# Broadcast rows of a half requested one half ahead, and the first stage's casts and low parts moved between ScalarE, GpSimd and VectorE

## The chip, the core and the metric

The kernel runs on one core of a Trainium2 chip (trn2). The core has five engines with instruction queues of their own: TensorE (PE in the rows, with its weight loads as PEld), VectorE (DVE), ScalarE (ACT), GpSimd (POOL) and SyncE (SP). All transfers between memory and the core's on-chip buffers are issued here from SyncE's queue. The metric is the device time of one execution in microseconds (us). The kernel before takes 1203.94 us, the median of three runs (1199.38 to 1205.58).

## The reference

A hybrid encoder layer is computed in float32 for two sequences, 512 and 256 tokens long, with 16 shared meta tokens in front of each. What matters for this change is the start: the layer norm, the input projection, and the preparation of the gated delta branch.

```
h = _layer_norm(concat(meta_tokens, x), ln_in_g, ln_in_b)      # 16 + 512 and 16 + 256 rows of 1024
proj = h @ w_in                                                # then split: c_q, c_kv, k_r, qkv, z, gates
qkv = silu(_centred_conv(qkv, conv_w)); q, k = _l2norm(q), _l2norm(k)
g, beta = -exp(a_log) * softplus(a + dt_bias), sigmoid(b)      # forward and backward
gc = cumsum(g) in chunks of 64;  decay = exp(gc_i - gc_j) below the diagonal
m = strict(k beta k^T * decay);  attn = (q k^T) * decay;  qg = q * exp(gc)
(solve with m + I per chunk, scan over the chunks, attention branch, w_out, feed-forward, two layer norms)
```

## The kernel before, in words

All 784 rows (16 meta, 512, 256) are handled together; the meta rows are computed once. The program is written as a sequence of loops, and a scheduler then fixes the order of the instructions on each engine from what they read and write; every engine, and SyncE's queue of transfers, works through its list in that order. Where a list stands at an instruction whose inputs or buffers are not ready, everything behind it on this engine waits.

First stage (lines 275 to 317). The rows are normalised in two halves, `s` = 0 and 1, of 400 and 384 rows. For each of eight slices `k` of 128 features TensorE transposes the slice (L308, L311), ScalarE applies gain and bias and writes `full` (called through `act`, L188), a cast writes the high part `hTh` (L316), and VectorE writes the low part `hTl = full - hTh` (L317). In the kernel before, the cast runs on VectorE for even `k` and on ScalarE for odd `k`. `hTh` and `hTl` together carry float32 accuracy through matrix multiplies of a narrower type.

Projection (`proj`, lines 320 to 333). A weight tile `wr` of 128 columns is loaded (L256), ScalarE casts it to its high part `wh` (L212), and the engine given as `eng` subtracts to its low part `wl` (L213). Then 48 matrix multiplies (L331) sum `wh*hTh + wh*hTl + wl*hTh`. In the kernel before, `eng` is GpSimd for the first projection (keys' rotary part and gates) and for the first pair of the delta branch, and VectorE for the pairs after it. `wh` and `wl` have two buffers each.

Gates (lines 338 to 431). The first projection's result is copied by ScalarE to `graw` (L346 to L349), VectorE forms `krt` (L350, L351), TensorE turns the gates (L354) and the rotary part (L437), VectorE computes the gate arithmetic, and rows of the result go to memory as `gD` (L420, L423).

Delta branch (lines 525 to 571). Four pairs of heads `j`; for each, two projections with convolution (`conv`, its sums on VectorE at L465), normalisation (`l2`), and a copy of the keys by tokens to `kt` (L508), which four transfers store to `vD` (L512). Then two halves, of seven chunks each. A half loads `x3`: five rows of `gD`, broadcast to 64 partitions, in two transfers (L542). `x3` has two buffers, so the load for a half waits until the half two before it has last read its own; that last reader is GpSimd's `ua` (L568). From `x3` VectorE forms `dc` (L547, L548), GpSimd masks it (L549, L550), ScalarE takes the exponential, and the products with the matrix multiplies of L561 are written to `LT` and, over three `ua` buffers, stored to `UD` (L571). Two stores belong to each `ua`.

What follows (the rest of the projections, the solve by chunks, the scan, attention, the output projection and the feed-forward) is not touched.

Of the kernel before, what the change touches and what calls it, by code (L numbers as in the profile page):

```python
# [5 lines left out]
F32 = mybir.dt.float32  # L6
# [7 lines left out]
P = 128  # L14
# [8 lines left out]
NCH = 14  # L23
# [114 lines left out]
def body(ctx, tc, I, O):  # L138
    nc = tc.nc
    V, S, G, T = nc.vector, nc.scalar, nc.gpsimd, nc.tensor  # L140
    ld = nc.sync.dma_start
# [108 lines left out]
    hTh = htp.tile([P, KT, NT], F32R, name="hTh")  # L250
# [24 lines left out]
    with ExitStack() as e0:  # L275
        xp = pool(e0, "xp", 1, "left")
        xs = pool(e0, "xs", 3, "left")
        xt = {}
        for t in (0, 1, 2, 3, 4, 5, 6):
            n = P if t else NM  # L280
            r0 = 0 if t == 0 else NM + (t - 1) * P
            x = xp.tile([n, D], F32, name=f"x{t}")
            ld(x, I["x"][r0:r0 + n, :])
            xt[t] = x
            if t == 3:
                ld(cst, I["consts"])
                ld(cols, I["cols"])
                w0 = load_w(0)
        m2 = xp.tile([P, 7, 2], F32, name="m27")
        G.memset(m2[:, 0], 1.0)  # L290
        for s, ts in enumerate((range(4), range(4, 7))):
            for t in ts:
                n = P if t else NM
                moments(xt[t], n, m2[:n, t], xs)
            tl = slice(ts[0], ts[-1] + 1)
            norm_factors(m2[:, tl], stat[:, tl], xs)
            for i, t in enumerate(ts):
                n = P if t else NM
                x, mv = xt[t], stat[:n, t]
                if i in (2,):  # L300
                    act(x, x, AF.Identity, bias=mv[:, 0:1], scale=mv[:, 1:2])
                else:
                    V.tensor_scalar(x, x, mv[:, 1:2], mv[:, 0:1], ALU.mult, ALU.add)
            for k in range(KT):
                ps = bank()
                ks = slice(k * P, (k + 1) * P)
                if s == 0:
                    T.transpose(ps[:, 0:NM], xt[0][:, ks], ident[:NM, :NM])  # L308
                o = 0 if s else NM
                for t in range(3):  # L310
                    T.transpose(ps[:, o + t * P:o + (t + 1) * P], xt[1 + s * 3 + t][:, ks], ident)  # L311
                w = H0 if s == 0 else HR
                cs = slice(s * H0, s * H0 + w)
                full = xs.tile([P, H0], F32, name="full", bufs=4)
                act(full[:, :w], ps[:, :w], AF.Identity, bias=col("lnb", k), scale=col("lng", k))
                (S.copy if k % 2 else V.tensor_copy)(hTh[:, k, cs], full[:, :w])  # L316
                V.tensor_sub(hTl[:, k, cs], full[:, :w], hTh[:, k, cs].bitcast(F32))  # L317


    def proj(ti, real=False, wr=None, eng=V):  # L320

        if wr is None:
            wr = load_w(ti)
        wh = wp.tile([P, KT, P], F32R, name="wh")
        wl = wp.tile([P, KT, P], F32R, name="wl")
        split(wr, wh, wl, eng=eng)
        ps = bank2()
        for s, (c0, c1) in enumerate(((NM if real else 0, H0), (H0, NT))):
            for k in range(KT):
                for i, (a, b) in enumerate(((wh, hTh), (wh, hTl), (wl, hTh))):  # L330
                    T.matmul(ps[:, s, :c1 - c0], lhsT=a[:, k, :], rhs=b[:, k, c0:c1],  # L331
                             start=(k == 0 and i == 0), stop=(k == KT - 1 and i == 2))
        return ps
# [1 line left out]

    eg = ExitStack()
    gp = pool(eg, "gp", 1, "left")
    ps = proj(0, wr=w0, eng=G)
    graw = gp.tile([P, GC], F32, name="graw")
    krt = gp.tile([64, NT], F32, name="krt")  # L340
    rk = gp.tile([64, NT], F32, name="rk")
# [10 lines left out]
    ps = bank()  # L352
# [42 lines left out]
    for nm, src in (("gcT", g), ("glT", g), ("bT", be)):  # L395
        o = gqp.tile([P, 2, 7, 2, 4], F32, name=nm)
        for rho in range(2):
            ps = bank()
            rows = slice(rho * 64, rho * 64 + 64)
# [12 lines left out]
    gD = dp.tile([2, 5, 56, 64], F32, name="gD")  # L412
    for i, src in enumerate((gcT[:, 0], gcT[:, 1], nbT[:, 0])):
        ps = bank()
# [19 lines left out]
    ps = bank2()  # L434
# [17 lines left out]
    def conv(ti, wi, eng=V, ceng=V):  # L452

        ps = proj(ti, eng=eng)
        xb = xbs[cnt[0] % 2]
        cnt[0] += 1
        S.copy(xb[:, 1:401], ps[:, 0, :H0])
        S.copy(xb[:, 532:548], ps[:, 0, 0:NM])
        S.copy(xb[:, 401:529], ps[:, 1, 0:128])
        S.copy(xb[:, 548:804], ps[:, 1, 128:HR])  # L460
        y = ps.rearrange("p a c -> p (a c)")[:, 0:803] if wi < 8 else ytile()
        S.mul(y, xb[:, 0:803], col("cw", wi * 4))
        for i in (1, 2, 3):
            if ceng is V:
                V.scalar_tensor_tensor(y, xb[:, i:i + 803], col("cw", wi * 4 + i), y, ALU.mult, ALU.add)  # L465
            else:
                t = ceng.tile([P, 803], F32, name="vt", bufs=2)
                S.mul(t, xb[:, i:i + 803], col("cw", wi * 4 + i))
                G.tensor_add(y, y, t)
        return y  # L470

    es = ExitStack()
    sp = pool(es, "sp", 1)
# [45 lines left out]
    def zgate(j):  # L519
# [2 lines left out]
        act(z[:, :NR].rearrange("p (a c) -> p a c", a=2), ps[:, :, :HR], AF.Silu)  # L522
        st(zD[j], z[:, :NR])

    for j in range(NPB):
        yk = conv(1 + 2 * j, 4 + j, eng=V if j else G)
        yq = conv(2 + 2 * j, j, eng=V if j else G)
        kq = sp.tile([P, 2, NCH, 64], F32, name="kq", bufs=2)
        ks, qs = (silu_pad(y, sp.tile([P, GC], F32, name="ks", bufs=2)) for y in (yk, yq))
        l2(ks, kq[:, 0], None)  # L530
        l2(qs, kq[:, 1], 0.125)
        tokens(kq[:, 0].rearrange("p n c -> p (n c)"), sp.tile([P, GC], F32, name="kt"), j, 0, bank)
        for half in range(2):
            n0 = half * 7
            ch = slice(n0, n0 + 7)
            rows = slice(j * NCH + n0, j * NCH + n0 + 7)

            x3 = sp.tile([P, 5, 7, 64], F32, name="x3", bufs=2)
            en = x3[:, 3:5]
            for h in range(2):  # L540
                hr = slice(h * 64, h * 64 + 64)
                ld(x3[hr].rearrange("p r n c -> p r (n c)"),  # L542
                   gD[h, :, rows].rearrange("r n c -> r (n c)").partition_broadcast(64))

            dc = sp.tile([P, 4, 7, 64], F32, name="dc", bufs=2)
            gc = bc(gcT[:, :, ch, j], 3, 64)
            V.tensor_sub(dc[:, 1:4:2], x3[:, 0:2], gc)  # L547
            V.tensor_sub(dc[:, 2], gc[:, 1], x3[:, 1])  # L548
            G.tensor_add(dc[:, 1:3], dc[:, 1:3], bc(bc(C("nf"), 1, 7), 1, 2))  # L549
            G.tensor_add(dc[:, 3], dc[:, 3], bc(C("nb"), 1, 7))  # L550
            act(dc[:, 1:4], dc[:, 1:4], AF.Exp)
            act(en, en, AF.Exp)
            G.tensor_mul(dc[:, 0], x3[:, 2], dc[:, 1])
            V.tensor_mul(dc[:, 2], dc[:, 2], bc(nbT[:, 1, ch, j], 2, 64))
            b = bds[half]
            S.copy(b[0:64, :, 64:128], kq[0:64, 0, ch, :])
            S.copy(b[64:128, :, 0:64], kq[64:128, 0, ch, :])
            for a, w in ((0, 4), (4, 3)):
                ps = bank()
                for i in range(w):  # L560
                    T.matmul(ps[:, i * P:(i + 1) * P], lhsT=b[:, a + i, :],  # L561
                             rhs=kq[:, :, n0 + a + i, :], start=True, stop=True)
                p4 = ps[:, :w * P].rearrange("p (n a c) -> p a n c", a=2, c=64)
                sl = slice(a, a + w)
                nj = slice((n0 + a) * 4 + j, (n0 + a + w - 1) * 4 + j + 1, 4)
                V.tensor_mul(LT[:, :, nj, :], bc(p4[:, 0], 1, 2), dc[:, 0:4:2, sl])
                ua = sp.tile([P, 2, 4, 2, 64], F32, name="ua", bufs=3)
                G.tensor_mul(ua[:, :, :w, 0, :], en[:, :, sl], bc(kq[:, 1, n0 + a:n0 + a + w, :], 1, 2))  # L568
                V.tensor_mul(ua[:, :, :w, 1, :], bc(p4[:, 1], 1, 2), dc[:, 1:4:2, sl])
                for r in range(2):  # L570
                    st(UD[r, n0 + a:n0 + a + w, :, j].rearrange("n p i c -> p n (i c)"), ua[:, r, :w].rearrange("p n i c -> p n (i c)"))  # L571
# [10 lines left out]
    for i0 in range(0, 64, 4):  # L582
        ps = bank()
# [141 lines left out]
    for i0 in range(0, 32, 4):  # L725
        ps = bank()
# [6 lines left out]
    for h in range(2):  # L733
        for b in range(2):
            rows = slice(h * 64 + b * 32, h * 64 + b * 32 + 32)
# [5 lines left out]
    for n0, r in ((0, 0), (96, 1), (16, 0), (80, 1), (32, 0), (64, 1), (48, 0), (56, 1)):  # L741
        w = 8 if n0 in (48, 56) else 16
# [15 lines left out]
        for h in range(2):  # L758
            rows = slice(h * 64 + 32, h * 64 + 64)
# [9 lines left out]
        for h in range(2):  # L769
            o = h * 64 + (32 if r else 0)  # L770
            R = slice(o, o + 32)
            c = 0 if r else 32
# [21 lines left out]
    for i in range(NBD):  # L794
        for l, nm in ((TBs, "TB"), (WBs, "WB"))[:2 if i < 2 else 1]:
            t = us.tile([P, 4, P], F32, name=f"{nm}{i}")
            for h in range(2):
                c = (1 - h) * 64 if nm == "TB" else h * 64
# [105 lines left out]
    for i in range(len(order) + 2):  # L904
        for _ in range(1):
            next(latg, None)
        if i < len(order):
            c, step = order[i]
# [5 lines left out]
        if i >= 2:  # L914
            c, step = order[i - 2]
# [4 lines left out]
            n = chains[c][1][step]  # L920
# [107 lines left out]
    for s in range(2):  # L1028
        ps = bank("v")
# [3 lines left out]
    for j in range(NPB):  # L1033
        for s in range(2):
            ps = bank("v")
            cs = slice(s * HR, (s + 1) * HR)
# [326 lines left out]
```

## Time and profile before

| | |
|---|---|
| median of three runs | 1203.94 us (1199.38 to 1205.58) |
| the profiled execution's own time | 1201.35 us |
| its span in the profile | 1199.4 us |
| mean granted TensorE clock | 0.967 of full speed |
| TensorE matrix multiplies busy | 1123.9 us, 94% of the span |
| VectorE busy | 831.6 us, 69% |
| ScalarE busy | 598.9 us, 50% |
| GpSimd busy | 156.6 us, 13% |

The span is the time from the first to the last instruction of one execution. A row of the timeline gives a start in us from the span's start, how long the instruction (or several alike, "x3") took, the engine, the line, and what is written from what; in brackets stands how long the engine was idle before it and what ended the wait. The chain that ended last follows the work back from the last instruction, at each step to what released it; it names, stretch by stretch, who was waited for. The rows by windows give each engine's busy time in a stretch, then the granted clock, the share of the transfer engines and GB/s.

### The profile page before, as it was taken

How to read it: one execution, taken by the hardware profiler on the slowest of the kernel's cores; microseconds unless marked ns; L12 is line 12 of the kernel's file. 1: busy time of each engine (PE TensorE's matmuls, PEld its weight loads, DVE VectorE, ACT ScalarE, POOL GpSimd, SP SyncE). 2: the span in 40 equal slices, each digit the busy share in tenths (PEclk: the TensorE clock that was granted, in tenths of full speed). 3: DMA queues.
4: the chain of work that ended last, by engine and by line, in shares of the span. 5: the costliest groups of instructions: out<-in, count | busy, mean ns of one | idle time of the engine just before them, and what ended most of it. 6: DMA issues, size and time to landing. Idle time of an engine off the chain costs nothing.

```text
span 1199.4 us, 18635 instructions
## 1 busy us (share of the span) xinstructions
PE 1123.9 (94%) x7116; PEld 974.5 (81%) x7116; DVE 831.6 (69%) x1358; ACT 598.9 (50%) x1054; POOL 156.6 (13%) x195
## 2 busy tenths in 40 slices
PE   5978888998999899998999899999998999999997
PEld 4877788998889876664677789999998888888885
DVE  7567668689677768778648699777764764494446
ACT  5475664333745656656534566555553533343330
POOL 2134465004513211000000000000000000000000
PEclk9998899999899989899999899999999999999999
DMA  5157764530478764334103025333324875566521
GB/s 209 50 117 182 196 171 130 126 113 31 146 253 238 214 188 124 102 98 158 45 18 106 18 71 179 129 123 123 124 88 145 306 229 177 176 206 203 179 91 52
DMA packets 107962, 168.94 MB, mean 141 GB/s; under 512 B 36242, under 2 KB 72850, under 8 KB 107874
## 3 DMA queue, kind: packets, MB, share of 16 engines
q1 hardware_dynamic: 107874, 167.76, 45.7%
q8 instruction: 56, 0.92, 0.3%
q14 instruction: 32, 0.26, 0.1%
HBM read 128.61 MB, written 39.11 MB: 140 GB/s over the span
## 4 chain that ended last, share of the span: by engine, by line
PE 77%; DVE 9%; DMA 6%; ACT 4%; issue 2%; SPq 1%; POOL 1%; DVEq 0%; ACTq 0%; POOLq 0%
PE w L1326 15%; PE w L1084 10%; PE b L1084 9%; PE d L331 7%; PE b L1326 7%; PE b L1146 5%; PE d L977 3%; PE c L1008 3%; DMA x<-gD 3%; PE b L837 2%; PE d L704 2%; PE b L853 2%; PE v L1005 2%; PE b L877 2%; PE b L870 2%
## 5 line engine op out<-in xcount | busy, mean ns | idle before, releaser
L1326 PE MATMUL w<-w2h,fh 128*128 128x512 f32 x768 | 185.1, 391 | 3.8 <-ACT fh L212 3.8
L1326 PEld LDWEIGHTS w<-w2h,fh 128*128 128x128 f32 x768 | 144.9, 189 | 34.3 <-ACT fh L212 4.1
L331 PE MATMUL d<-hTh,wl 128*128 128x384 f32 (+1 forms) x352 | 123.9, 352 | 3.3 <-DVE wl L213 3.3
L331 PE MATMUL d<-hTh,wh 128*128 128x384 f32 (+1 forms) x352 | 125.1, 355 | 1.4 <-ACT ks L188 1.4
L331 PE MATMUL d<-hTl,wh 128*128 128x384 f32 (+1 forms) x352 | 125.1, 355 | 0.0
L213 DVE TENSOR_TENSOR w2h<-LT,w2h 128x1024 fp32r<-128x1024 f32 x64 | 77.6, 1224 | 48.7 <-ACT w2h L212 48.7
L212 ACT CAST w2h<-LT 128x1024 fp32r<-128x1024 f32 x64 | 66.6, 1049 | 75.4 <-PE b L1326 28.8
L1326 PE MATMUL b<-w2h,fh 128*128 128x512 f32 x384 | 96.4, 389 | 0.0
L1326 PEld LDWEIGHTS b<-w2h,fh 128*128 128x128 f32 x384 | 72.3, 188 | 15.1
L331 PEld LDWEIGHTS d<-hTh,wh 128*128 128x128 f32 x352 | 67.6, 192 | 5.8 <-issue 3.3
L331 PEld LDWEIGHTS d<-hTh,wl 128*128 128x128 f32 x352 | 67.6, 192 | 5.8 <-DVE wl L213 3.7
L331 PEld LDWEIGHTS d<-hTl,wh 128*128 128x128 f32 x352 | 67.6, 192 | 2.6 <-issue 1.5
L213 DVE TENSOR_TENSOR fh<-fr,fh 128x768 fp32r<-128x768 f32 x32 | 30.5, 957 | 55.9 <-ACT fh L212 55.9
L212 ACT CAST fh<-fr 128x768 fp32r<-128x768 f32 x32 | 26.7, 839 | 76.0 <-PE w L1326 38.7
L212 ACT CAST w1h<-LT 128x512 fp32r<-128x512 f32 x50 | 30.8, 620 | 41.2 <-PE w L1084 20.9
L1146 PE MATMUL b<-woh,mh 128*128 128x512 f32 x96 | 42.2, 448 | 5.2 <-ACT woh L212 3.1
L977 PE MATMUL d<-kt,q 128*128 128x512 f32 (+1 forms) x96 | 46.6, 582 | 0.3 <-ACT p L188 0.2
L213 DVE TENSOR_TENSOR w1l<-LT,w1h 128x512 fp32r<-128x512 f32 x50 | 34.4, 689 | 12.6 <-ACT w1h L212 12.6
L1008 PE MATMUL c<-pt,vt 128*64 128x512 f32 (+3 forms) x96 | 42.2, 536 | 0.6 <-ACT pt L1007 0.6
L857 DVE TENSOR_TENSOR YZ<-U,b 64x512 f32<-64x512 f32 x52 | 35.5, 683 | 7.6 <-PE b L853 6.9
L834 ACT COPY YZ<-U 64x512 f32<-64x512 f32 x52 | 32.1, 617 | 17.3 <-issue 11.3
L978 DVE TENSOR_REDUCE mx<-d 128x1 f32<-128x512 f32 (+1 forms) x48 | 28.7, 599 | 16.7 <-PE d L977 16.5
(473 smaller groups left out, 2810.4 us busy)
## 6 DMA issues: line engine op xcount, KB each, us to landing
LT<-in_w_ff SPq DMA_DIRECT2D x85, 512.0 KB, 3.8
FD<-LT SPq DMA_DIRECT2D x16, 768.0 KB, 3.7
fr<-FD SPq DMA_DIRECT2D x32, 384.0 KB, 3.7
wr<-in_w_in SPq DMA_DIRECT2D x22, 512.0 KB, 3.5
x<-gD SPq DMA_DIRECT2D x16, 560.0 KB, 6.2
KV<-vD SPq DMA_DIRECT2D x26, 256.0 KB
U<-UD SPq DMA_DIRECT2D x26, 256.0 KB, 5.3
w1x<-in_w_ff SPq DMA_DIRECT2D x12, 512.0 KB, 4.5
```

Source lines behind the costliest of these rows:

```text
L212: S.copy(hi, src)
L213: return (eng or V).tensor_sub(lo, src, hi.bitcast(F32))
L331: T.matmul(ps[:, s, :c1 - c0], lhsT=a[:, k, :], rhs=b[:, k, c0:c1], start=(k == 0 and i == 0), stop=(k == KT - 1 and i == 2))
L704: T.matmul(ps[:, s, :HR], lhsT=a[:, k], rhs=b[:, cs], start=(k == 0 and i == 0), stop=(k == 2 and i == 2))
L834: S.copy(YZ[h][rows], U[rows, :, :, 1])
L857: V.tensor_sub(YZ[h][rows], U[rows, :, :, 0], wv[rows])
L977: T.matmul(ps[:, :w], lhsT=q[:, qs], rhs=kt[:, k0:k0 + w], start=True, stop=True)
L978: V.tensor_reduce(mx[:, 0, t:t + 1], ps[:, :w], AX.X, ALU.max)
L1008: T.matmul(po[:m, :nq], lhsT=Vs[j][:, t0 + bi, :m], rhs=pt[:, :nq], start=(bi == 0), stop=(bi == ntl - 1))
L1084: x = T.matmul(ps[:, :HR], lhsT=a[:, k, :], rhs=b[:, k, :], start=(k == 0 and i == 0), stop=(k == HQ - 1 and i == 2))
L1146: outp = T.matmul(ps, lhsT=x[:, k, :], rhs=y[:, cs], start=(k == 0 and i == 0), stop=(k == 3 and i == 2))
L1326: T.matmul(po[g][h], lhsT=a[:, i_, qs], rhs=b[:, cs], start=(n_ == 0 and j == 0), stop=(n_ == len(seq) - 1 and j == 2))
```

## The change

Three things are edited. The cast to `hTh` runs on ScalarE for all eight slices. The low part `wl` of the first projection and of the first pair's two projections is formed on VectorE instead of GpSimd. And the loads of `x3` move into a function `lines`, which is called once before the loop for the first half and then, in each half, for the half that follows, in front of this half's own work and stores.

```
-                (S.copy if k % 2 else V.tensor_copy)(hTh[:, k, cs], full[:, :w])
+                S.copy(hTh[:, k, cs], full[:, :w])
...
-    ps = proj(0, wr=w0, eng=G)
+    ps = proj(0, wr=w0)
...
+    def lines(j, half):
+
+        rows = slice(j * NCH + half * 7, j * NCH + half * 7 + 7)
+        x3 = sp.tile([P, 5, 7, 64], F32, name="x3", bufs=2)
+        for h in range(2):
+            hr = slice(h * 64, h * 64 + 64)
+            ld(x3[hr].rearrange("p r n c -> p r (n c)"),
+               gD[h, :, rows].rearrange("r n c -> r (n c)").partition_broadcast(64))
+        return x3
+
+    x3n = lines(0, 0)
     for j in range(NPB):
-        yk = conv(1 + 2 * j, 4 + j, eng=V if j else G)
-        yq = conv(2 + 2 * j, j, eng=V if j else G)
+        yk = conv(1 + 2 * j, 4 + j)
+        yq = conv(2 + 2 * j, j)
...
-            x3 = sp.tile([P, 5, 7, 64], F32, name="x3", bufs=2)
+            x3 = x3n
             en = x3[:, 3:5]
-            for h in range(2):
-                hr = slice(h * 64, h * 64 + 64)
-                ld(x3[hr].rearrange("p r n c -> p r (n c)"),
-                   gD[h, :, rows].rearrange("r n c -> r (n c)").partition_broadcast(64))
+            if 2 * j + half < 7:
+                x3n = lines(j + half, 1 - half)
```

Since a scheduler sets the order, the lists of the built programs say what moves. ScalarE in the second half of the first stage, from the first `full` of 384 rows to the cast of the second weight pair; the list before:

```order
L188 ACTIVATE full<-b,cols 128x384 x4
L316 CAST hTh<-full 128x384
L188 ACTIVATE full<-b,cols 128x384
L316 CAST hTh<-full 128x384
L188 ACTIVATE full<-b,cols 128x384 x2
L316 CAST hTh<-full 128x384
L188 ACTIVATE full<-b,cols 128x384
L188 ACTIVATE ea<-gv 128x16
L316 CAST hTh<-full 128x384
L212 CAST wh<-wr 128x1024
```

Four casts stand among eight `full`. The list now, over the same stretch:

```order
L188 ACTIVATE full<-b,cols 128x384 x3
L316 CAST hTh<-full 128x384
L188 ACTIVATE full<-b,cols 128x384
L316 CAST hTh<-full 128x384 x3
L188 ACTIVATE full<-b,cols 128x384 x3
L316 CAST hTh<-full 128x384 x2
L188 ACTIVATE full<-b,cols 128x384
L316 CAST hTh<-full 128x384 x2
L188 ACTIVATE ea<-gv 128x16
L212 CAST wh<-wr 128x1024
```

Eight casts stand there, the last two right in front of the weight cast. In the first half ScalarE's list gains four casts in the same way, and VectorE's loses its four and gains two subtractions of `wl`; a third `wl` now stands on VectorE just ahead of `krt` (L350).

SyncE's queue in the delta branch, from the second half of pair `j` = 0 to pair 2; the names `x_994`, `x_1208` and `x_1243` are the `x3` of the second half of pair 1 and of the two halves of pair 2. The list before:

```order
L571 DMA UD<-ua 128x4x128 x2
L542 DMA x_994<-gD 64x5x448 x2
L256 DMA wr<-in_w_in 128x1024
L571 DMA UD<-ua 128x3x128 x2
L256 DMA wr<-in_w_in 128x1024 x2
L542 DMA x_1208<-gD 64x5x448 x2
L512 DMA vD<-kt 64x7x64 x4
L571 DMA UD<-ua 128x4x128 x2
L571 DMA UD<-ua 128x3x128 x2
L571 DMA UD<-ua 128x4x128 x2
L571 DMA UD<-ua 128x3x128 x2
L542 DMA x_1243<-gD 64x5x448 x2
```

The same stretch now, where `x_962`, `x_997` and `x_1211` are the three tiles, and L531 and L578 are the old L542 and L571:

```order
L578 DMA UD<-ua 128x4x128 x2
L531 DMA x_962<-gD 64x5x448 x2
L256 DMA wr<-in_w_in 128x1024
L578 DMA UD<-ua 128x3x128 x2
L256 DMA wr<-in_w_in 128x1024 x2
L512 DMA vD<-kt 64x7x64 x4
L531 DMA x_997<-gD 64x5x448 x2
L578 DMA UD<-ua 128x4x128 x2
L578 DMA UD<-ua 128x3x128 x2
L578 DMA UD<-ua 128x4x128 x2
L578 DMA UD<-ua 128x3x128 x2
L531 DMA x_1211<-gD 64x5x448 x2
```

The two loads for the first half of pair 2 stand behind the four stores of `vD`, where they stood in front of them. At every other place SyncE's queue has the order it had. Around the same place ScalarE's second copy to `kt` now precedes the first product of the convolution (L462), and on VectorE one sum of the convolution (L465) changes places with one pair of products (L566, L569). Beyond that the lists of all engines are the same but for a few neighbours.

## Rows read from the trace of the kernel before

**Rows 1.** Windows: length, busy PE, PEld, DVE, ACT, POOL, clock, DMA share, GB/s
```profile
12.00:25.00 13.00, 12.43 (x55) 9.99 (x56) 12.86 (x28) 9.19 (x18) 6.15 (x8) 1.00 0.48 175
25.00:35.00 10.00, 8.57 (x50) 6.64 (x49) 7.27 (x14) 8.00 (x15) 0.00 (x0) 1.00 0.07 18
...
38.60:40.80 2.20, 2.20 (x7) 2.11 (x7) 2.02 (x5) 0.79 (x2) 0.00 (x0) 0.50 0.69 225
...
184.00:260.00 76.00, 76.00 (x461) 74.77 (x461) 60.37 (x80) 32.54 (x56) 16.28 (x20) 0.98 0.52 135
```
**Rows 2.** Timeline of VectorE in the first half of the first stage
```profile
17.96 0.56 DVE L317 TENSOR_TENSOR hTl<-full,hTh 128x400 fp32r<-128x400 f32 x1
...
19.87 2.63 DVE L317 TENSOR_TENSOR hTl<-full,hTh 128x400 fp32r<-128x400 f32 x1
```
**Rows 3.** Timeline of GpSimd in the same stretch
```profile
18.83 3.24 POOL L213 TENSOR_TENSOR wl<-wr,wh 128x1024 fp32r<-128x1024 f32 x1 [3.17 <-ACT wh L212]
```
**Rows 4.** Line 316, all its instructions: ns min/median/max, first and last start
```profile
L316 DVE CAST hTh<-full x8: 301/360/540, 15.7 to 32.0; 128x400 fp32r<-128x400 f32 x4, 128x384 fp32r<-128x384 f32 x4
L316 ACT CAST hTh<-full x8: 516/524/532, 16.1 to 32.9; 128x400 fp32r<-128x400 f32 x4, 128x384 fp32r<-128x384 f32 x4
```
**Rows 5.** Timeline of VectorE, a weight's low part formed there
```profile
50.64 1.23 DVE L213 TENSOR_TENSOR wl<-wr,wh 128x1024 fp32r<-128x1024 f32 x1 [5.57 <-PE b L403]
```
**Rows 6.** Timeline of ScalarE, second half of the first stage
```profile
27.07 2.36 ACT L188 ACTIVATE full<-b,cols 128x384 f32<-128x384 f32 x4 [0.83 <-PE b L311]
29.31 0.52 ACT L316 CAST hTh<-full 128x384 fp32r<-128x384 f32 x1
29.71 0.69 ACT L188 ACTIVATE full<-b,cols 128x384 f32<-128x384 f32 x1
...
32.95 0.52 ACT L316 CAST hTh<-full 128x384 fp32r<-128x384 f32 x1
```
**Rows 7.** Chain that ended last, 31 to 40 us: start, length, what
```profile
31.00 3.57 PE d L331 x19
...
34.64 1.04 ACT wh L212
...
36.72 0.58 DVE krt L350
```
**Rows 8.** Timeline of SyncE's queue: start, issue time, transfer
```profile
101.61 1.47 SPq L542 DMA_DIRECT2D x<-gD  x2
...
126.56 1.25 SPq L542 DMA_DIRECT2D x<-gD  x2
127.92 3.03 SPq L512 DMA_DIRECT2D vD<-kt  x4
```
**Rows 9.** Timeline of ScalarE at the copies by tokens of pair 1
```profile
124.48 0.63 ACT L508 COPY kt<-b 128x512 f32<-128x512 f32 x1
...
125.82 0.53 ACT L508 COPY kt<-b 128x384 f32<-128x384 f32 x1
```
**Rows 10.** Timeline of VectorE at the arrival of broadcast rows
```profile
111.42 1.09 DVE L547 TENSOR_TENSOR dc<-x,gcT 128x896 f32<-128x896 f32 x1 [4.22 <-DMA x<-gD]
...
134.66 1.09 DVE L547 TENSOR_TENSOR dc<-x,gcT 128x896 f32<-128x896 f32 x1 [1.85 <-DMA x<-gD]
```
**Rows 11.** Timeline of GpSimd behind the arrival at 134.66
```profile
135.83 1.45 POOL L550 TENSOR_TENSOR dc<-dc,cst 128x448 f32<-128x448 f32 x1 [5.02 <-DVE dc L547]
137.51 1.01 POOL L568 TENSOR_TENSOR ua<-x,kq 128x384 f32<-128x384 f32 x1 [0.23 <-DMA UD<-ua]
```
**Rows 12.** Chain that ended last, 100 to 178 us: start, length, what
```profile
102.26 9.04 DMA x<-gD
...
140.73 7.86 DMA x<-gD
...
157.01 2.93 PE d L331 x8
...
170.02 7.20 DMA x<-gD
```

More of the change, by code (lines that the diff above doesn't have):

```diff
@@ L535, in body @@
             ch = slice(n0, n0 + 7)
-            rows = slice(j * NCH + n0, j * NCH + n0 + 7)
-            x3 = sp.tile([P, 5, 7, 64], F32, name="x3", bufs=2)
+            x3 = x3n
             en = x3[:, 3:5]
-            for h in range(2):
-                hr = slice(h * 64, h * 64 + 64)
-                ld(x3[hr].rearrange("p r n c -> p r (n c)"),
-                   gD[h, :, rows].rearrange("r n c -> r (n c)").partition_broadcast(64))
+            if 2 * j + half < 7:
+                x3n = lines(j + half, 1 - half)
             dc = sp.tile([P, 4, 7, 64], F32, name="dc", bufs=2)
```

## The prediction

> **What bounds the kernel now.** I read the page's busy times first: TensorE is at work for most of the span, so a change pays or costs only where TensorE is made to wait. Then the chain that ended last, for the stretch the edits touch. From 31 to 40 us it goes through TensorE's multiplies of the first projection (31.00, ending at 34.57), ScalarE's weight cast and VectorE's `krt` [rows 7]. From 100 to 178 us it goes three times through a load of broadcast rows, 9.04, 7.86 and 7.20 us long [rows 12]. Behind 184 us TensorE is busy for 76.00 of 76 us [rows 1]: what arrives there late stays late, for the lists fix the order and there is no pause to absorb a delay. Third I read the engines' timelines around these places, and last the built lists, which say what really moves.
>
> **First stage, first half.** Off VectorE go four casts of 0.36 us (1.4) [rows 4]. Off goes also a stall: one `hTl` took 2.63 us where its like takes 0.56 [rows 2], while GpSimd formed `wl` from 18.83 to 22.07 [rows 3]; with GpSimd empty that is 2.1 less. On it come two `wl` of 1.23 us, 2.5 [rows 5]. VectorE alone would reach the second half's normalisation, near 25 us, about 1.0 us sooner. ScalarE gets four casts of 0.52 us, 2.1, in a window in which it is idle for 13.00 - 9.19 = 3.8 us [rows 1, 4]; but the low part of the eighth slice waits for the last of them and stands in VectorE's list ahead of the last normalisation factor (L234). So the bounds are 1.0 us gained (ScalarE keeps up) and 2.1 us lost (none of its casts is hidden). I take a gain of 0.3, nearer to VectorE's own count, since ScalarE has idle time for all four casts.
>
> **First stage, second half.** Here ScalarE is the fuller engine, 8.00 of 10 us against VectorE's 7.27 [rows 1]. From 27.07 four `full` take 2.36, 0.59 each, and a cast delays what follows by 0.40, from 29.31 to 29.71 [rows 6]. Eight of each make 4.7 + 3.2 = 7.9 us, so the last cast ends at 35.0, where it ended at 33.47 [rows 6]. Behind it come one low part (0.56) and its two multiplies (0.2 each [rows 7]), so TensorE's first projection ends at 36.0, not 34.57: 1.4 us late. The bounds are 0 (TensorE late anyway) and 2.1 (four casts at full length). The third `wl` starts when the weight cast ends (34.64 + 1.04 = 35.68 [rows 7]) and now stands ahead of `krt` on VectorE; 35.68 + 1.23 = 36.9 against 36.72, another 0.2. If `krt` had to wait for it in full, 1.2. The first stage therefore loses 1.4 + 0.2 - 0.3 = 1.3 us. Its bounds are -1.0 and 2.1 + 2.1 + 1.2 = +5.4.
>
> The Trainium skill (Perfetto Trace Analysis, Optimizing Scalar/DVE Operations) speaks against this half of the edit: where VectorE has a fast mode for an operation it does it faster, and work is handed to ScalarE when VectorE is saturated. The trace agrees on the first part, 0.36 against 0.52 us [rows 4], and VectorE is not saturated in the second half, 7.27 of 10 us [rows 1]. By the rule the price would be the difference of the durations, four times 0.16 or 0.6 us; by the rows it is the whole length on ScalarE, since ScalarE ends last.
>
> **The broadcast rows.** The loads do not come a half earlier. SyncE's list keeps its order at seven of eight halves, as the scheduler had moved the loads up already, and a load still waits for GpSimd's last read of the tile two halves before. At the one other place, the first half of pair 2, the two loads fall behind the four stores of `vD`. The stores need the second copy to `kt`, which ended at 126.35 and now follows straight on the first: 125.11 and about 0.4 make 125.5 [rows 9]. Issuing the four takes 3.03 us [rows 8], so the loads go out at 128.6 instead of 126.56, 2.0 later. From the first issue to VectorE's first use it took 134.66 - 126.56 = 8.1 us [rows 8, 10]. The load at 101.61, which went out shortly behind four such stores, took 111.42 - 101.61 = 9.8 [rows 8, 10]. I take 8.1, since that load had two stores of `UD` ahead of it too; 9.8 would add 1.7. What waits: VectorE's `dc` at 134.66, GpSimd's mask behind it, and behind the mask in GpSimd's list the `ua` that frees `x3` for the second half of pair 2. The mask ended at 137.28 and `ua` started at 137.51, held by a store of `UD` [rows 11], so 0.2 of the 2.0 is hidden and the next load, on the chain at 140.73 [rows 12], goes out 1.8 us late. TensorE waits behind that one until 157.01. The bounds are 0 (the `UD` store hides it) and 1.8 + 1.7 = 3.5. The swaps around it (one sum of the convolution behind a pair of products) I cost at nothing: VectorE waits 1.85 us for the rows there already [rows 10], and loses at most a 1.09-us instruction if that cover goes.
>
> The Trainium skill (DMA: Bandwidth & Descriptors, Queues, rings and completion order) says that a transfer engine takes descriptors in the order of its ring. By this rule the loads would begin only when the data of the four stores is through, and this term would be the upper bound, 3.5 us and not 1.8. The load at 101.61 bears that out in part; its 9.8 us hold two more stores as well.
>
> **Sum.** 1.3 + 1.8 = 3.1 us later. On the profiled execution, 1201.35 us (1199.4 of span and 2 around it), that is 1204.5. The median of the runs is 2.6 above this execution, so the forecast is 1207, 0.26% above 1203.94. About 0.5%, 6 us, is what a measurement of this kernel can tell from no change; the forecast lies inside.
>
> **Rivals.** First, slower through TensorE's clock. After the pause behind 34.57 the granted clock was 0.50 from 38.6 to 40.8, the lower level of 1.2 GHz [rows 1], and at 157.01 eight multiplies took 2.93 us [rows 12] where 19 take 3.57, or 1.5 for eight [rows 7]: 1.4 us for one such stretch. All three new waits (behind the last cast, at the first half of pair 2, at the second) lengthen pauses of TensorE. If each brings one more slow stretch that multiplies wait on, 4.3 is added: 3.1 + 4.3, or 1211. It decides from two stretches on, 3.1 + 2.9 = 6.0. For it speaks that both pauses were followed by the low clock; against it, that these stretches are there already and may only shift.
>
> Second, the casts hide. If ScalarE keeps up in both halves, the first stage gains the 1.0 us of VectorE, and with the queue's 1.8 the sum is +0.8: 1205. For it speaks ScalarE's 3.8 idle microseconds in the first half; against it, the count in the second.
>
> Third, the change does what it says and the rows of a half are there when it begins. The three loads on the chain are worth 9.04 + 7.86 + 7.20 = 24.1 us [rows 12]; since the mask and the `UD` stores are late next, about half would come through: 1192. Against it stands SyncE's list.
>
> **How the numbers follow.** The forecast gets 0.49, the clock 0.20, the hidden casts 0.24, the earlier rows 0.07. Slower by over 0.5% (above 1210) is most of the clock's 0.20 and the upper end of the forecast's bounds, 0.21 together. Faster by over 0.5% (below 1198) is the third rival and a little of the second, 0.08. Within 0.5% is 0.71. The range starts from the forecast and the clock: with both terms near their upper bounds, or two slow stretches, 1212; with the first stage at its lower bound, no cost of the queue, and a median as much below 1203.94 as the profiled execution is, 1200. Beyond lie the earlier rows and three slow stretches together with large terms.
>
> **What would show it.** In the profile of the changed kernel no `hTl` takes over 0.7 us in the first half; ScalarE's last cast of the first stage ends near 35 us, and TensorE's first projection near 36. The two loads for pair 2 go out about 2 us after the first of the four `vD` stores would have let them, and VectorE waits longer at that `dc`. The chain still goes through three loads of broadcast rows of 7 to 10 us. The prediction is wrong if these loads leave the chain, if TensorE's first projection ends by 34.6, or if the second load of pair 2 is issued no later, counted from `kt`, than before.

## The result, and the profile after

The changed kernel took 1210.39 us (median of six executions), the kernel before, run beside it, 1202.07: a ratio of 1.006 [1.0034, 1.0085]. In a second series (e1 below) it took 1206.58 (twelve executions) against 1202.74: 1.0031 [1.0021, 1.0042]. By the ratios the change costs 7.2 us in the first series and 3.7 in the second. The forecast was 1207, 3.1 us later; the two intervals share only a narrow strip at 1.004, so the size is known to some 2 us, and the first median lies 3.4 above the forecast and inside its range. Ratios leave out the executions in which TensorE's clock was low throughout (0.56 in the profiled one of the six), so the rows below are those of a second profile, an execution of 1205.0 us with a span of 1203.0.

The first stage, ScalarE's timeline, beside [rows 6]:

```profile
26.97 1.80 ACT L188 ACTIVATE full<-b,cols 128x384 f32<-128x384 f32 x3 [0.82 <-PE b L311]
...
29.63 1.34 ACT L316 CAST hTh<-full 128x384 fp32r<-128x384 f32 x3
30.86 1.82 ACT L188 ACTIVATE full<-b,cols 128x384 f32<-128x384 f32 x3
...
33.92 0.96 ACT L316 CAST hTh<-full 128x384 fp32r<-128x384 f32 x2
```

ScalarE goes from cast to `full` to cast without a gap, and the last cast ends at 34.88; before, it ended at 33.47. VectorE's timeline, beside [rows 2]:

```profile
17.94 0.55 DVE L317 TENSOR_TENSOR hTl<-full,hTh 128x400 fp32r<-128x400 f32 x1
...
21.79 1.55 DVE L317 TENSOR_TENSOR hTl<-full,hTh 128x400 fp32r<-128x400 f32 x3 [0.56 <-ACT hTh L316]
24.22 0.58 DVE L317 TENSOR_TENSOR hTl<-full,hTh 128x400 fp32r<-128x400 f32 x1 [0.42 <-ACT hTh L316]
24.91 0.81 DVE L303 TENSOR_SCALAR x<-x,stat 128x1024 f32<-128x1024 f32 x1
```

The `hTl` of 2.63 us is gone, but VectorE now waits for ScalarE's casts, and the second half's normalisation starts at 24.91. In the kernel before that row reads

```profile
25.00 1.54 DVE L303 TENSOR_SCALAR x<-x,stat 128x1024 f32<-128x1024 f32 x2
```

so this execution gains 0.1 us in the first half; a second profile of the same kernel (e6) gains nothing. The chain of waits from 35 us, beside [rows 7]:

```profile
35.10 0.97 PE d L331 x4
...
36.10 1.05 ACT wh L212
...
38.32 0.57 DVE krt L350
```

The first projection ends at 36.07 (34.57 before), and `krt` starts 1.60 us later than before.

Then the transfers. SyncE's queue, beside [rows 8]:

```profile
128.81 2.96 SPq L512 DMA_DIRECT2D vD<-kt  x4
132.28 1.26 SPq L531 DMA_DIRECT2D x<-gD  x2
...
145.32 1.25 SPq L531 DMA_DIRECT2D x<-gD  x2
```

ScalarE, beside [rows 9]:

```profile
127.78 1.00 ACT L508 COPY kt<-b 128x512 f32<-128x512 f32 x2
```

The four stores go out as soon as the second copy is done, and the two loads follow half a microsecond behind them. Counted from the start of the first copy to `kt`, the loads go out after 4.50 us (132.28 - 127.78), before after 2.08 (126.56 - 124.48): 2.4 later. It is the stores that held them and not the buffer, whose last reader on GpSimd was done at 129.83:

```profile
126.69 3.14 POOL L575 TENSOR_TENSOR ua<-x,kq 128x512 f32<-128x512 f32 x2 [1.09 <-DVE kq L498]
```

VectorE's arrivals, beside [rows 10]:

```profile
114.71 1.09 DVE L554 TENSOR_TENSOR dc<-x,gcT 128x896 f32<-128x896 f32 x1 [4.83 <-DMA x<-gD]
140.73 1.09 DVE L554 TENSOR_TENSOR dc<-x,gcT 128x896 f32<-128x896 f32 x1 [4.25 <-DMA x<-gD]
154.05 1.09 DVE L554 TENSOR_TENSOR dc<-x,gcT 128x896 f32<-128x896 f32 x1 [2.69 <-DMA x<-gD]
```

GpSimd behind the second of them, beside [rows 11]:

```profile
141.90 1.47 POOL L557 TENSOR_TENSOR dc<-dc,cst 128x448 f32<-128x448 f32 x1 [7.52 <-DVE dc L554]
143.34 1.01 POOL L575 TENSOR_TENSOR ua<-x,kq 128x384 f32<-128x384 f32 x1
```

The wait at the first half of pair 2 grew from 1.85 to 4.25 us, and `ua` no longer waits for a store of `UD`. The chain, beside [rows 12], now goes through four loads:

```profile
104.90 9.69 DMA x<-gD
132.94 7.67 DMA x<-gD
145.94 7.98 DMA x<-gD
176.16 7.46 DMA x<-gD
```

### The profile page after: what moved, and what is told of

Same layout as the page of the kernel before. It is cut to its first block, busy times and chain, and to the rows that moved or that the text cites. A ratio compares the mean times of both kernels' runs of the same rounds, so it can differ in the third digit from the quotient of the medians.

```text
span 1823.8 us, 18636 instructions
## 1 busy us (share of the span) xinstructions
PE 1787.9 (98%) x7116; PEld 1216.5 (67%) x7116; DVE 829.8 (45%) x1353; ACT 605.1 (33%) x1062; POOL 144.0 (8%) x192
## 4 chain that ended last, share of the span: by engine, by line
PE 96%; DVE 1%; ACT 1%; DMA 0%; issue 0%; DVEq 0%; SPq 0%; ACTq 0%
PE d L331 17%; PE w L1333 16%; PE w L1091 11%; PE b L1091 10%; PE b L1333 8%; PE b L1153 6%; PE c L1015 3%; PE d L984 3%; PE b L844 2%; PE d L711 2%; PE b L860 2%; PE v L1012 2%; PE b L884 1%; PE b L877 1%; PE b L568 1%; PE b L492 1%
## 5 line engine op out<-in xcount | busy, mean ns | idle before, releaser
L1333 PE MATMUL w<-w2h,fh 128*128 128x512 f32 x768 | 306.8, 577 | 3.8 <-ACT fh L212 3.8
L331 PE MATMUL d<-hTh,wh 128*128 128x384 f32 (+1 forms) x352 | 177.0, 503 | 0.0
L331 PE MATMUL d<-hTl,wh 128*128 128x384 f32 (+1 forms) x352 | 175.4, 498 | 0.0
L331 PE MATMUL d<-hTh,wl 128*128 128x384 f32 (+1 forms) x352 | 174.1, 495 | 0.0
L1333 PE MATMUL b<-w2h,fh 128*128 128x512 f32 x384 | 158.7, 576 | 0.0
L984 PE MATMUL d<-kt,q 128*128 128x512 f32 (+1 forms) x96 | 71.1, 854 | 0.0
L1015 PE MATMUL c<-pt,vt 128*64 128x512 f32 (+3 forms) x96 | 68.3, 819 | 1.1 <-ACT pt L1014 1.1
L1153 PE MATMUL b<-wol,mh 128*128 128x512 f32 x96 | 55.8, 583 | 0.0
L1153 PE MATMUL b<-woh,ml 128*128 128x512 f32 x96 | 54.6, 581 | 0.0
L1012 PEld LDWEIGHTS v<-cst,p 128*128 128x128 f32 x160 | 24.2, 164 | 43.4 <-issue 35.3
```

Of the source, the lines that this page charges most:

```text
L984: T.matmul(ps[:, :w], lhsT=q[:, qs], rhs=kt[:, k0:k0 + w], start=True, stop=True)
L1012: T.transpose(ps[:, t * P:(t + 1) * P], res[t0 + t][:, c0:c0 + P], ident)
L1015: T.matmul(po[:m, :nq], lhsT=Vs[j][:, t0 + bi, :m], rhs=pt[:, :nq], start=(bi == 0), stop=(bi == ntl - 1))
L1153: outp = T.matmul(ps, lhsT=x[:, k, :], rhs=y[:, cs], start=(k == 0 and i == 0), stop=(k == 3 and i == 2))
L1333: T.matmul(po[g][h], lhsT=a[:, i_, qs], rhs=b[:, cs], start=(n_ == 0 and j == 0), stop=(n_ == len(seq) - 1 and j == 2))
```

## The experiments

**Lists.** Two parts of the edit need no run. The new `lines` function alone gives, on all five engines, the list of the kernel before. The casts and low parts alone give the list of the changed kernel. So the stores moved ahead of the loads with the casts and low parts (with the casts alone too, as e4 shows); asking for the rows earlier in the code changed nothing.

**The changed kernel itself (e1_after).** 

> The changed kernel as it is, for a profile at the normal clock. Theory (both terms as forecast, too small in size): 4 to 10 us slower than before; TensorE's first projection ends 1.5 to 3 us later than 34.6, and the wait for the broadcast rows of pair 2's first half is 2 to 4 us longer. Rival (clock): the two waits are as long as forecast, 1.3 and 1.8 us, and the rest of the loss lies in stretches at the lower granted clock that the kernel before has not. Rival (late): the loss appears behind 260 us, in the untouched part.

Measured: 1.0031 [1.0021, 1.0042], or 3.7 us, a little less than the theory's 4 to 10. The first projection ends 1.5 us later and the wait at pair 2 is 2.4 us longer, both near the theory's lower ends. The loss does not appear behind 260 us: at 247 us this execution is 7.4 us late already (shown below).

**The queue's order put back (e2).** The four stores of pair 1 become a function that is called behind the loads for pair 2.

```diff
+        if (j, w) == (1, 0):
+            return stores
...
+            if late is not None and half == 1:
+                for y in late():
+                    tc.add_manual_dep(y.ins, xl[0].ins.name, NOSYNC, reason="behind the loads")
```

> The changed kernel, with the four vD stores of pair 1 behind the loads of pair 2's first half again, as before; every other list is that of the changed kernel. Theory: the first stage's share alone remains, 1 to 4 us slower than before, and it is 2 to 4 us faster than the changed kernel. Rival (the queue costs nothing, the first stage everything): as slow as the changed kernel within 1 us. Rival (the first stage costs nothing): as fast as before within 1 us.

Measured: 1204.68 us, 1.0012 [0.9999, 1.0024]. VectorE's arrivals:

```profile
115.21 1.09 DVE L562 TENSOR_TENSOR dc<-x,gcT 128x896 f32<-128x896 f32 x1 [4.89 <-DMA x<-gD]
138.92 1.09 DVE L562 TENSOR_TENSOR dc<-x,gcT 128x896 f32<-128x896 f32 x1 [1.95 <-DMA x<-gD]
152.78 1.09 DVE L562 TENSOR_TENSOR dc<-x,gcT 128x896 f32<-128x896 f32 x1 [2.77 <-DMA x<-gD]
```

The wait at pair 2 is 1.95 again. By the medians e2 is 1.9 us faster than e1 and 1.4 slower than the kernel before; what is left I put down to the first stage. By the times alone neither part is far from the noise: the intervals of e1 and e2 touch, and that of e2 reaches 1.

**Casts shared as before in the first half only (e3).**

```diff
- S.copy(hTh[:, k, cs], full[:, :w])
+ (S.copy if k % 2 or s == 1 else V.tensor_copy)(hTh[:, k, cs], full[:, :w])
```

> The changed kernel with the casts of the first stage's first half shared between VectorE and ScalarE as before (second half all on ScalarE, low parts on VectorE, queue order as before the change). Theory: the second half's casts carry the first stage's cost, so this takes the same time as the changed kernel with the queue order set back, within 1 us. Rival (the first half carries it): 1 to 2 us faster than that one.

Measured: 1204.67 us, 1.0013 [0.9998, 1.0028]; its queue has the loads in front, as in e2, and it costs what e2 costs. The first half's casts cost nothing that these runs can tell, to some 1.5 us.

**Casts alone, low parts left on GpSimd (e4).**

```diff
- (S.copy if k % 2 else V.tensor_copy)(hTh[:, k, cs], full[:, :w])
+ S.copy(hTh[:, k, cs], full[:, :w])
```

> The kernel before with the casts all on ScalarE; low parts stay on GpSimd, loads as before. Its queue has the stores ahead of the loads as the changed kernel has, and a few loads near the end of the scan in another order. Theory: as slow as the changed kernel or 1 to 2 us slower, since the 2.1-us stall of VectorE behind GpSimd stays and ScalarE's casts are there. Rival (the low parts on VectorE carry the cost, through the wait of krt behind wl): 2 to 4 us faster than the changed kernel.

Measured: 1205.49 us, 1.0027 [1.0014, 1.0041]. Its queue has the stores in front, and its arrivals show it:

```profile
110.53 1.09 DVE L547 TENSOR_TENSOR dc<-x,gcT 128x896 f32<-128x896 f32 x1 [4.03 <-DMA x<-gD]
136.63 1.09 DVE L547 TENSOR_TENSOR dc<-x,gcT 128x896 f32<-128x896 f32 x1 [4.33 <-DMA x<-gD]
```

By the time the casts alone and the whole change can't be told apart. The casts bring both costs: `krt` starts at 38.00, late as in e1, and the stores overtake the loads.

**Both kernels profiled again (e5, e6).** 

> The kernel before once more, for a second profile of it: how far the places at which I read the shift of the changed kernel move by themselves between two executions. In the first profile the multiplies behind the first projection's copies start at 38.7 us and run at the lower clock until about 41.1; the long row of 113 multiplies starts at 240.2 and the first score multiply at 420.5. If the low-clock stretch at 39 us belongs to the order of the work, it is again 2 to 3 us long here. If it falls as it likes, its length differs by more than 2 us, and then the 6.5 us that the changed kernel shows there are no cost of the change.

The execution took 5586 us and its profile tells nothing; so there is one usable profile of the kernel before, and this question had to be answered from the other kernels.

> The changed kernel once more, for a second profile. In the first the low clock behind the first projection lasts from 38.7 to about 45.2 us, the row of 113 multiplies starts at 247.6 (7.4 us later than before), and the first score multiply at 425.5 (5.0 later). If these are costs of the change, they come again within 1 us, and the 7 us late at 250 us again shrink to 3 to 5 by 445 us. If they are chance, the second profile differs from the first by as much as the two profiles of the kernel before differ from each other.

Measured: 1205.85 us. Its row of 113 multiplies starts at 245.75, 1.8 us earlier than in the first profile, more than the 1 us that the expectation allows a cost of the change, and its low clock is shorter. The window from 36 to 46 us (the clock is the third figure from the end), first of the kernel before:

```profile
36.00:46.00 10.00, 9.37 (x40) 7.37 (x41) 7.69 (x24) 2.60 (x9) 2.52 (x5) 0.83 0.16 53
```

of e1:

```profile
36.00:46.00 10.00, 8.02 (x29) 6.47 (x28) 7.87 (x23) 3.36 (x9) 0.00 (x0) 0.66 0.18 53
```

of e6, the same list:

```profile
36.00:46.00 10.00, 8.02 (x35) 6.15 (x34) 7.74 (x22) 3.36 (x9) 0.00 (x0) 0.83 0.17 53
```

and of e8 (below), which has the first stage of the kernel before:

```profile
36.00:46.00 10.00, 9.32 (x32) 7.22 (x32) 7.69 (x24) 2.19 (x8) 2.68 (x5) 0.66 0.17 53
```

With the same list e1 has 0.66 and e6 has 0.83, and the old first stage shows both values too. e4 shows 1.00. So the list does not fix the length of this stretch. Whether the change makes the longer one more frequent, these few profiles can't say.

**TensorE's pause filled (e7).**

```diff
+    for i in range(5):
+        f = T.matmul(fl[:, :H0 - NM], lhsT=hTh[:, i % KT, 0:P], rhs=hTl[:, i % KT, NM:H0], start=True, stop=True)
```

Five multiplies, whose result is not read, stand ahead of the gates' transposes; a sixth stands behind them.

> The changed kernel with six multiplies of 384 columns, whose result nobody reads, put into TensorE's pause behind the first projection: five ahead of the gate rows' transposes, one behind them. Everything else stands in the same order. They need 6 x 0.18 = 1.1 us of a pause of 2.9 us (35.98 to 38.94 less 0.7 of transposes), so by themselves they delay nothing. Theory: the low clock at 38.7 to 45.2 us follows the pause; a shorter pause shortens it, the place that the row of 21 multiplies reaches at 63.1 us comes 1 to 1.5 us earlier, and the ratio to the kernel before falls from 1.003 to about 1.002. Rival: the clock falls there all the same, the multiplies run as slowly as in the changed kernel, and the ratio stays at 1.003.

Measured: 1203.97 us, 1.0016 [1.0002, 1.0029]. The clock stayed at 1.00 from 36 to 46 us in the profile, and the row of 21 multiplies started at 60.62 (63.07 in e1, 62.02 in e6). The ratio came out where the theory put it, but the intervals of e7 and e1 overlap, and e4 kept the full clock with the pause unfilled. So it is not settled that the filling did it.

**The loads cut in two (e8, and e9 again).** e8 is the kernel before with the change's function `lines`, and in it two tiles instead of one; `xe` takes the two rows that are held to the half's end.

```diff
+        x3 = sp.tile([P, 3, 7, 64], F32, name="x3", bufs=2)
+        xe = sp.tile([P, 2, 7, 64], F32, name="xe", bufs=2)
+        for x, r0, r1 in ((x3, 0, 3), (xe, 3, 5)):
...
+            x3, en = x3n
```

The same cut without `lines` gives the list of e8 on all five engines, so what follows comes from the cut and not from asking earlier.

> The kernel before with its broadcast loads cut in two tiles: three rows of gates that are free again once the decay tile is made, and two rows that are held until the half's end, as all five were. In the built order each next three-row load then stands ahead of the half's remaining stores. Casts and low parts as before. Theory: the loads are on the chain in four places with 7 to 10 us each, because the buffer comes free late and not because of the order in which the code asks for them; freed earlier they leave the chain, and the time falls by 5 to 15 us, to 1188 to 1198. Rival: the chain takes the next wait at once (the other loads, the stores, the engines' own 30 us a half) and the time is within 3 us of the kernel before.

Measured: 1181.20 us, 0.9807 [0.9787, 0.9826], 21 us faster than the kernel before and beyond the 5 to 15 of the theory. VectorE's longest wait from 60 to 200 us (what waits for what, total, times, longest), in the kernel before:

```profile
DVE dc L547 <- DMA x<-gD: 23.3, 7, 6.6
```

and in e8:

```profile
DVE dc L555 <- DMA x<-gD: 7.7, 2, 6.8
```

The two that are left are the first of all, in which no earlier buffer is waited for. GpSimd waits longer for the stores of `UD` instead, before

```profile
POOL ua L568 <- DMA UD<-ua: 3.1, 3, 2.6
```

and in e8

```profile
POOL ua L576 <- DMA UD<-ua: 15.0, 3, 7.6
```

How much of the 21 us had come through by 400 us is shown by one line of a later stage (ns min/median/max of an instruction, first and last start in us), before

```profile
L704 PE MATMUL d<-lh,uh x48: 331/338/441, 346.9 to 395.3; 128*128 128x384 f32 x48
```

and in e8

```profile
L712 PE MATMUL d<-lh,uh x48: 331/338/450, 338.0 to 388.0; 128*128 128x384 f32 x48
```

There e8 is 7 to 9 us ahead; of its 18.8 us at the end of the span (1180.6 against 1199.4) the other 10 to 11 arise behind, where the cut gave the engines other lists. SyncE's queue of e8, where both three-row loads stand in front of the stores of pair 1:

```profile
115.25 1.24 SPq L533 DMA_DIRECT2D x<-gD  x2
...
118.41 1.23 SPq L533 DMA_DIRECT2D x<-gD  x2
...
125.98 2.67 SPq L512 DMA_DIRECT2D vD<-kt  x4
```

> The kernel before with its loads cut in two, once more, beside the two kernels that carry parts of the change on top of it, so that the three share a chip. Expected as measured: a ratio of 0.981 to the kernel before, about 1180 us.

Measured: 1181.46 us over five executions, 1180.52 over the four that the ratio counts: 0.9823 [0.9801, 0.9844].

**Parts of the change on top of it (e10, e11), and low parts alone (e12).** e10 is the changed kernel with the cut of e8, e11 is e8 with

```diff
- ps = proj(0, wr=w0, eng=G)
+ ps = proj(0, wr=w0)
```

and the same at the two `conv` calls, and e12 has this last edit alone.

> The changed kernel with its loads cut in two in the same way: all casts on ScalarE, all low parts on VectorE, and each next three-row load standing ahead of the half's stores. Theory: the loads no longer stand behind the four stores of pair 1, so of the change's two costs (first stage about 1.5 to 2 us, queue about 2 to 3 us) only the first is left: 1 to 2.5 us slower than the kernel before with its loads cut in two. Rival: the queue never mattered, and all of 3 to 4 us is still there. A second rival: with another order of the work from 100 us on, the 3 us either way that an order brings by itself hide both.

Measured: 1191.10 us, 0.9906 [0.9889, 0.9923], 10.6 us slower than the four executions of e9 beside it: a miss for both theories, and more than the 3 us of the second rival. At the line shown above e10 is 2 to 4 us ahead of e8:

```profile
L712 PE MATMUL d<-lh,uh x48: 331/338/442, 336.0 to 384.0; 128*128 128x384 f32 x48
```

It is behind in the output projection, e8:

```profile
L1154 PE MATMUL b<-woh,mh x96: 388/394/798, 529.7 to 661.7; 128*128 128x512 f32 x96
```

and e10:

```profile
L1154 PE MATMUL b<-woh,mh x96: 388/394/799, 533.6 to 670.2; 128*128 128x512 f32 x96
```

So in these two executions the loss arises behind 384 us, where the scheduler gave the two kernels different lists; the waits of the casts and of the queue in the first 200 us did not make it. Which instructions did, no run tells.

> The kernel before with its loads cut in two, the casts shared as before and only the low parts of the first three projections moved from GpSimd to VectorE. Theory: the cost of the change's first stage is ScalarE's, in the casts of the second half, so this part alone costs nothing: within 1.5 us of the kernel before with its loads cut in two. Rival: the low parts on VectorE stand ahead of the rotary multiplies and of the second half's low parts and carry the cost: 1.5 to 2.5 us slower than it.

Measured: 1186.67 us, 0.9879 [0.9851, 0.9906], 6.2 above the four executions of e9, with single executions from 1182.38 to 1194.68: a miss for the theory and for its rival. `krt` starts at 36.61, no later than before (36.72): the low parts cost nothing where they stand. Its lists differ from those of e8 on every engine; that this other order makes the difference is not shown by a run of its own.

> The kernel before with the low parts of its first three projections on VectorE and nothing else changed; from 45 us on the order of the work then is another on every engine, so what is compared is the time alone and the stretch up to 60 us. Theory: with the casts shared, the row of 21 multiplies at 60 us starts no later than before, and the time is within 3 us of the kernel before, the two or three stores that stand elsewhere deciding its sign. Rival: the low parts cost 1.5 to 2 us at 60 us too.

Measured: 1206.41 us, 1.0037 [1.0020, 1.0054]; `krt` at 36.79, so here too the first stage is not late. The 3.8 us are over the 3 that the theory allowed the other order; nothing else of the edit is left to explain them, but no run shows where they arise.

## Why the prediction was right

Both terms of the forecast stood at the places that it gave them: 3.1 was forecast, and 3.7 measured in the second series. That the sum came so near is in part luck, since the second term was too small, and part of the delay was absorbed again behind 400 us. In the first series, 7.2 us later, half of the loss would be without an account; its only profile can't be used.

*First stage, forecast 1.3.* Measured 1.6 at `krt` in e1. From the second half's normalisation (24.91 in e1) to the last cast it takes 9.95 to 9.97 us in all seven profiles in which ScalarE makes that half's casts, and 8.45 to 8.47 in the four in which they are shared: 1.5 (forecast 1.4). From the last cast's end to `krt` it is 3.44 us in e1, 3.36 in e4 with `wl` on GpSimd, 3.25 before: 0.1 for the third `wl` (forecast 0.2), and 0.1 that comes without it. The gain of 0.3 in the first half did not come. From the first normalisation (L303) to that of the second half it takes 13.95 us in the kernel before and 13.91 in e1, but 14.33 in e6, the same kernel: the stall is gone, but VectorE now waits for ScalarE's casts (0.56 and 0.42 us in e1). By the medians e2 and e3 give 1.4 and 1.6 us, with intervals from about -0.1 to 2.9 and -0.2 to 3.4. The Trainium skill (Perfetto Trace Analysis, Optimizing Scalar/DVE Operations) says only that VectorE is faster where it has a fast mode, and that ScalarE may take over work from a saturated VectorE; a price it does not state, and the 0.6 us were my own reading. Measured are 1.5 for four casts, 0.38 each: close to the 0.40 by which a cast delays what follows it on ScalarE, and less than the 0.52 that it lasts.

*Broadcast rows, forecast 1.8.* Starts of VectorE's first `dc` in the fourth, fifth and sixth of the eight halves (before: [rows 10]):

| | 4th | 5th | 6th | 4th to 5th | 4th to 6th |
|---|---|---|---|---|---|
| before | 111.42 | 134.66 | 148.71 | 23.24 | 37.29 |
| e1, stores in front | 114.71 | 140.73 | 154.05 | 26.02 | 39.34 |
| e6, the same kernel | 113.49 | 139.86 | 153.17 | 26.37 | 39.68 |
| e4, stores in front | 110.53 | 136.63 | 149.79 | 26.10 | 39.26 |
| e7, stores in front | 112.25 | 138.69 | 153.03 | 26.44 | 40.78 |
| e2, loads in front | 115.21 | 138.92 | 152.78 | 23.71 | 37.57 |
| e3, loads in front | 114.80 | 138.14 | 152.13 | 23.34 | 37.33 |

With the stores in front, the fifth comes 2.8 to 3.2 us later than before (forecast 2.0) and the sixth 2.0 to 3.5 (forecast 1.8); with the loads in front both come 0.0 to 0.5 later. The loads went out 2.4 us later and not 2.0, since the queue stood still for 0.5 us behind the stores. Then 0.7 to 0.9 was hidden behind the fifth in e1, e4 and e6, where I had 0.2: the wait for the store of `UD` as forecast, and the issue of the next two loads, which took 1.25 us in e1 where it took 1.86 before. In e7 nothing was hidden. From issue to use the loads took 8.4 to 8.9 us with the stores in front (8.45 in e1) and 8.1 to 8.6 with the loads in front, near the 8.1 that I took and not the 9.8. The rule of the Trainium skill (DMA: Bandwidth & Descriptors, Queues, rings and completion order) is that descriptors are taken in the order of the ring. That the loads would then begin only behind the stores' data, for 3.5 us, was my reading; the section says too that a later descriptor may finish its write before an earlier one. Here the stores in front show in about 0.3 of the 8.4 to 8.9 us.

The term went on growing where the forecast had ended. In the eighth half (177.34 before, 183.74 in e1), counted from the fourth as in the table, e1, e4, e6 and e7 are 2.9 to 3.6 us late, e2 and e3 0.1 and 1.0.

*"What arrives there late stays late."* Right up to 400 us; behind that, in e1, not. The chain, then TensorE at the first score multiplies, then the chain again, in the kernel before:

```profile
240.17 20.08 PE d L331 x113
...
420.48 2.71 PE L967 MATMUL d<-kt,q 128*128 128x16 f32 x12 [3.90 <-DMA KV<-vD]
...
443.10 1.25 PE d L967 x12
```

in e1:

```profile
247.58 20.08 PE d L331 x113
...
425.50 1.48 PE L974 MATMUL d<-kt,q 128*128 128x16 f32 x12 [1.82 <-DMA q<-QD]
...
446.74 1.25 PE d L974 x12
```

and in e6:

```profile
245.75 20.08 PE d L331 x113
...
426.31 2.71 PE L974 MATMUL d<-kt,q 128*128 128x16 f32 x12 [3.15 <-DMA KV<-vD]
...
448.67 1.25 PE d L974 x12
```

e6 is 5.6 us late at 240 us and at 443. e1 is 7.4 late, and then 3.6. So there is a pause that absorbs a delay: ahead of the first score multiplies TensorE waited 3.90 us for a load in the kernel before and 1.82 in e1, which takes 2.1 off. Another 1.2 comes from the clock, 12 multiplies in 1.48 us at the full clock where the kernel before shows 2.71. The prediction had looked no further than 260 us. A single profile can so mistake the clock of two stretches for the change's cost or gain; the terms above were read between neighbouring places for that reason.

*The clock rival.* Half right. A longer slow stretch of TensorE did stand behind the first pause in e1, e2 and e3, and e1 has up to 3.0 us at the row of 21 multiplies (63.07 against 60.06), of which 1.6 is the stage. But e6 has the length of the kernel before, and e8, with the old first stage, has that of e1. So the longer stretch is no fixed price of the change; how much of the median it carries is open, and e7, which cost 1.9 us by its ratio with the full clock there, leaves room for some 2 us. A second place, which the rival did not name, shows more. Behind the loads of the eighth half TensorE starts on nine multiplies, in the kernel before

```profile
183.53 2.60 PE d L331 x9
```

and in e1

```profile
189.91 3.37 PE d L331 x9
```

with a clock of 0.91 and 0.83 from 180 to 200 us. e4, e6 and e7 have 3.37 too, e3 has 2.71, and e2 has the full clock there: 0.8 us more, each time with the stores in front.

*The hidden casts* fell with the 1.5 us that the second half's casts cost in every profile.

*The change does what it says.* Rightly given little, since the load waits for its buffer. Its price, half of the three loads' 24.1 us, is borne out roughly by e8, where the buffer did come free early. VectorE's wait fell by 23.3 - 7.7 = 15.6 us, the stores of `UD` that I had named as late next took a part of it (3.1 us of waiting before, 15.0 in e8), and 7 to 9 us had come through by 395 us. The rest of the 21 arises behind, in other lists, and e10 to e12 show how much an order can do.

## What to carry to other kernels

A load that waits for a buffer is not made earlier by asking for it earlier; look for who reads the tile last, and give the rows that are held long a tile of their own. Work moved to the engine that ends last delays the end by what it adds to that engine's own row (0.38 us a cast here), whatever the other engine gains. And where a scheduler sets the order, a local edit is to be judged by the lists of the whole program: the stores that overtook two loads 90 us later cost about as much here as the casts themselves, and the same edit on the faster kernel cost 10.6 us, in its profile all behind 384 us.

## What the runs showed of the hardware

The same list was followed by TensorE's low clock for very different times: the mean clock from 36 to 46 us was 0.83 in one execution and 0.66 in another. If it was at 0.50 or 1.00 throughout, these are an estimated 3.4 and 6.8 us at the lower level. With the pause partly filled (e7), or with another list (e4), there was none. I had expected its length to follow from the pause.

Behind four stores of 0.7 us of issue each (2.96 us together in e1), two loads went out 2.4 us later, and then took 8.45 us from issue to use, where loads in front took 8.1 to 8.6. What a place in the queue costs lay here in the issue and hardly in the transfer.
